# Seven of eight gate tiles of a hybrid encoder block by a seven-product block scheme, and the last head's attention in pieces among the u products (one core)

## The chip, the core and the metric

The kernel runs on one core of a Trainium2 chip. The metric is device time in microseconds of one execution of the whole program. Five engines work side by side, each through its own queue in order: TensorE (PE in the profile, its weight loads PEld), VectorE (DVE), ScalarE (ACT), GpSimd (POOL) and SyncE (SP, which here only issues DMAs). Tiles live in SBUF, and TensorE writes its results into PSUM, which has eight banks of 128 x 512 float32.

## What is computed

One layer of an encoder on a sequence of S = 512 tokens with D = 1024 features, all float32:

```
n = rms_norm(h, norm_mix_pre);  proj = n @ w_in        # 1024 x 7680
z_gmlp (u, v), q, k, v, gates = split(proj)
y_a = u * (w_spatial @ LN(v) + b_spatial)              # after gelu, chunks of 128
y_b = dilated window attention, 3 groups x 4 heads, mixed by softmax denominators
g_a, g_b = split(sigmoid(gates + b_gate))              # 1024 columns each
merged = g_a * (y_a @ w_branch_a) + g_b * (y_b @ w_branch_b)
h = h + rms_norm(merged @ w_out)
h = h + rms_norm(relu(rms_norm(h) @ w_up)**2 @ w_down)
```

## The kernel before

Every large product keeps float32 precision with three fast products. A matrix is split into a rounded high part (type float32r, an ACT copy) and the rest (a DVE subtraction; lines 75 and 76 in `wsplit`, 80 and 81 in `split_into`), and `mm3` (lines 83 to 87) issues high x high, high x low and low x high into one PSUM bank. So one 128-deep step of a product of 128 x 128 weights with 512 moving columns is three matmuls.

The work runs in stages. The input is normed and transposed into `nh`, `nl` (eight slices of 128 features), then v of attention group 0 and of groups 1 and 2 is projected, then q and k of four heads; head h-1 is attended inside the projections of head h (`project_qk`, line 262). `mix(h)` joins the softmax statistics, and `attend(h)` (lines 371 to 415) transposes the probabilities in four rounds through the one PSUM bank with the tag "T", copies them out, and accumulates 12 matmuls of group 0 and the strided ones of the others into the bank "y".

Then comes the part that the change touches. `token_major` for v of the gMLP (line 466) fills the four banks of the tag "acc"; half-way through its text stands `attend(NH - 1)`, the last head. `evac_v` (lines 456 to 464) applies gelu to each of the four banks and norms them. The u loop (lines 468 to 483) makes four feature tiles of 24 matmuls each in the two banks of the tag "S", applies gelu (`gelu2`, lines 447 to 452), multiplies by the spatial product `pg` and splits the result into `yah`, `yal`.

The gate loop (lines 494 to 514) goes over eight column tiles d. For each, two gate products (branches 0 and 1) of 8 x 3 matmuls with 512 moving columns go through a sigmoid with a bias; two branch products of 4 x 3 matmuls are multiplied with the gates and added, and the sum is split into `mh[:, d]`, `ml[:, d]`. Weights come in slabs of 256 columns. After that w_out, w_up and w_down follow; the w_up stage (lines 707 to 738) already uses the seven-product scheme for 14 pairs of column tiles.

The order of instructions on each engine is not the order of the text. A list scheduler places an instruction when its inputs, its buffers and its engine are free in its own time model, the earlier text first. `tc.issue_after(x)` only forbids that TensorE instructions of the block stand ahead of x. A tile waits for its buffer until every reader of the former tile there is done; pools of a closed stack give their SBUF to later pools, which wait for the old tiles in the same way. So the `mpool` of line 489 waits for what the `attn` stack (closed in line 486: `v0h`, `v0l`, `v12` and the probabilities) held.

## Time and profile before

| what | value |
|---|---|
| median of 3 runs (range) | 828.11 us (827.78 to 830.46) |
| the profiled execution's own time | 827.73 us |
| its span, first to last instruction | 826.0 us |
| TensorE busy | 809.8 us (98%) |
| VectorE, ScalarE, GpSimd busy | 493.1 us (60%), 348.9 us (42%), 80.3 us (10%) |
| granted TensorE clock | 1.000 |

In the profile's rows, `L85 PE MATMUL pf<-nh,hi` is a matmul issued by line 85 that writes tile `pf` from `nh` and `hi`; then come the shape, the count, and busy time and mean duration. Matmuls overlap in the pipeline: one of 512 columns lasts 393 ns in its row, but the next starts earlier. What a matmul costs is therefore the distance from one start to the next, read from the timeline or from the count in a window that is wholly busy. A bracket at the end of a timeline row is the idle time ahead of it, and who ended it.

### The profile page before, as it was taken

What the parts mean: (1) busy time and instruction counts of PE and PEld (TensorE: products, weight loads), DVE (VectorE), ACT (ScalarE), POOL (GpSimd) and SP (SyncE); (2) the same over time, 40 slices, a digit from 0 to 9 for tenths busy, and PEclk for the clock granted to TensorE, in tenths of its full rate; (3) what the DMA queues carried; (4) which work ended last, traced back from release to release, by engine and by line L of the source; (5) the groups of instructions that cost most, each with busy time, mean ns of one, the idle gap of its engine ahead of it and who ended that gap; (6) DMA issues with size and microseconds to landing.
All of it is one profiled execution on the core that took longest, in us unless ns stands there. A gap on an engine that the chain in (4) does not pass through costs nothing.

```text
span 826.0 us, 10927 instructions
## 1 busy us (share of the span) xinstructions
PE 809.8 (98%) x4371; PEld 704.8 (85%) x4371; DVE 493.1 (60%) x831; ACT 348.9 (42%) x561; POOL 80.3 (10%) x82
## 2 busy tenths in 40 slices
PE   7999999999999999999999999999999999999997
PEld 5899888888888778888888889999999888888885
DVE  6432788978775637433336579988887533333324
ACT  6322243435344353232326455666666533223312
POOL 2000123232215200000001100000000000000000
PEclk9999999999999999999999999999999999999999
DMA  9433233322213131431436221533333733222202
GB/s 306 137 103 97 67 92 102 85 69 82 74 52 121 60 102 53 152 102 51 153 107 199 102 78 52 153 102 103 103 103 120 263 102 102 89 79 91 100 1 102
DMA packets 70372, 86.90 MB, mean 105 GB/s; under 512 B 2033, under 2 KB 57489, under 8 KB 70322
## 3 DMA queue, kind: packets, MB, share of 16 engines
...
q14 instruction: 16, 0.13, 0.1%
...
## 4 chain that ended last, share of the span: by engine, by line
PE 96%; ACT 1%; DVE 1%; DMA 1%; issue 0%; SPq 0%; DVEq 0%; POOLq 0%; ACTq 0%
PE pf L87 12%; PE pf L86 12%; PE pf L85 12%; PE pacc L699 11%; PE pd L85 9%; PE pd L86 9%; PE pd L87 9%; PE ptp L699 5%; PE pv L85 4%; PE pv L87 4%; PE pv L86 4%; PE py L413 1%; PE psb L313 1%; PE pu L86 1%; PE pu L87 1%; PE pu L85 1%
## 5 line engine op out<-in xcount | busy, mean ns | idle before, releaser
L87 PE MATMUL pf<-nh,lo 128*128 128x512 f32 x352 | 138.2, 393 | 0.0
L86 PE MATMUL pf<-nl,hi 128*128 128x512 f32 x352 | 138.1, 392 | 0.0
L85 PE MATMUL pf<-nh,hi 128*128 128x512 f32 x352 | 137.8, 392 | 0.0
L85 PE MATMUL pd<-hl,hh 128*128 128x512 f32 x224 | 87.1, 390 | 1.0 <-ACT hh L80 1.0
L86 PE MATMUL pd<-hl,hh 128*128 128x512 f32 x224 | 87.2, 389 | 0.0
L87 PE MATMUL pd<-hl 128*128 128x512 f32 x224 | 86.0, 389 | 0.0
L87 PEld LDWEIGHTS pf<-nh,lo 128*128 128x128 f32 x352 | 66.1, 188 | 13.5 <-issue 0.2
L85 PEld LDWEIGHTS pf<-nh,hi 128*128 128x128 f32 x352 | 66.1, 188 | 13.5 <-issue 0.2
L86 PEld LDWEIGHTS pf<-nl,hi 128*128 128x128 f32 x352 | 66.1, 188 | 13.3
L699 PE MATMUL pacc<-nt,hl 128*128 128x256 f32 x504 | 68.2, 280 | 0.4 <-DVE hl L81 0.3
L81 DVE TENSOR_TENSOR hl<-hid,hh 128x512 fp32r<-128x512 f32 x28 | 19.3, 693 | 79.3 <-ACT hh L80 78.9
L699 PEld LDWEIGHTS pacc<-nt,hl 128*128 128x128 f32 x504 | 63.1, 188 | 0.9 <-DVE hl L81 0.5
L254 POOL TENSOR_TENSOR sw<-sw,rope 32x512 f32<-32x512 f32 x24 | 42.3, 1761 | 174.6 <-DVE sw L252 157.5
L80 ACT ACTIVATE hh<-hid 128x512 fp32r<-128x512 f32 x28 | 17.6, 630 | 92.9 <-PE pd L86 92.9
L85 PE MATMUL pv<-hi,nh 128*128 128x512 f32 x128 | 50.9, 402 | 0.4 <-ACT nh L80 0.4
L87 PE MATMUL pv<-hi,nl 128*128 128x512 f32 x128 | 51.2, 401 | 0.0
L86 PE MATMUL pv<-lo,nh 128*128 128x512 f32 x128 | 51.1, 399 | 0.0
L85 PEld LDWEIGHTS pd<-hl,hh 128*128 128x128 f32 x224 | 42.0, 188 | 10.4 <-ACT hh L80 1.4
L87 PEld LDWEIGHTS pd<-hl 128*128 128x128 f32 x224 | 42.0, 188 | 8.7
L86 PEld LDWEIGHTS pd<-hl,hh 128*128 128x128 f32 x224 | 42.0, 188 | 8.6
L81 DVE TENSOR_TENSOR hl<-dnw,hl 128x1024 fp32r<-128x1024 f32 x32 | 39.2, 1226 | 13.8 <-ACT hl L80 13.8
L75 ACT ACTIVATE hi<-qkw 128x1024 fp32r<-128x1024 f32 x24 | 25.4, 1058 | 49.4 <-PE pf L86 25.8
...
## 6 DMA issues: line engine op xcount, KB each, us to landing
upw<-in_w_up_dram SPq DMA_DIRECT2D x16, 1024.0 KB, 5.6
dnw<-in_w_down_dram SPq DMA_DIRECT2D x16, 1024.0 KB, 4.8
qkw<-in_w_in_dram SPq DMA_DIRECT2D x24, 512.0 KB, 4.6
gw<-in_w_in_dram SPq DMA_DIRECT2D x8, 1024.0 KB, 5.2
slab<-in_w_in_dram SPq DMA_DIRECT2D x6, 1024.0 KB, 12.8
wow<-in_w_out_dram SPq DMA_DIRECT2D x4, 1024.0 KB, 4.9
w0raw<-in_w_in_dram SPq DMA_DIRECT2D x4, 512.0 KB, 6.6
uw<-in_w_in_dram SPq DMA_DIRECT2D x2, 1024.0 KB, 5.8
```

What stands on the lines that cost most here:

```text
L75: nc.scalar.activation(hi, raw, AF.Copy)
L80: nc.scalar.activation(hi, src, AF.Copy)
L81: nc.vector.tensor_tensor(lo, src, hi.bitcast(F32), op=ALU.subtract)
L85: nc.tensor.matmul(ps, ah, bh, start=start, stop=False)
L86: nc.tensor.matmul(ps, ah, bl, start=False, stop=False)
L87: return nc.tensor.matmul(ps, al, bh, start=False, stop=stop)
L254: nc.gpsimd.tensor_tensor(sw, sw, rope[:, 1], op=ALU.mult)
L313: nc.tensor.matmul(ps[:, rr, g - 1], got["q", g][:, r], got["k", g][:, r], start=True, stop=True)
L413: nc.tensor.matmul(o, v12[:, g, r, hs], ptb[r // 2][:, r % 2, g], start=False, stop=(r == 3 and g == 1), skip_group_check=True)
L699: nc.tensor.matmul(ps, a[:, j], b[:, j], start=first and not (j or m), stop=(j == KH - 1 and m == 2), skip_group_check=True)
```

## The change

- **Gates.** Tile d = 0 stays as it was. For each d from 1 to 7, the two gate column tiles (branch 1 and branch 0) and the two halves of 256 tokens form a 2 x 2 block product, which is made from seven products of half depth (4 k-steps) with 256 moving columns in place of eight. The weights get four sums (`seven`), the moving side gets four combinations once (`four_sums`, on a rebuilt float32 copy `nf` of the normed input), and PSUM results are combined by DVE and ACT. Product 4 of a pair and its two branch products (`branches`) come after product 6 of the next pair. The branch products use the PSUM banks "T" and "y". Weights come in 128-column pieces.
- **Last head.** `attend` becomes a generator with four yields; the pieces for head 3 are traced after the fourth and the eighth k-step of the u tiles. The u tiles move from the banks "S" to the banks "acc", the spatial products and the small set-up transposes to the banks "S".
- **Memory.** The pool `gpool` moves to the right side, a 160-byte spacer goes, and the scratch for GpSimd's dynamic DMAs is set to 8192 bytes, which leaves that much more per partition for tiles.

```diff
-    spacer(right, 160, "yedge")
...
-        ps = psA.tile([P, S], F32, name="pf", tag=tag, bufs={"acc": 4, "S": 2}[tag])
+        ps = psA.tile([P, S], F32, name="pf", tag=tag, bufs={"acc": 4, "S": 2, "T": 1, "y": 1}[tag])
...
+    def attend_steps(h):
...
             pta_l.append(lo)
+            yield
...
+        turn_b(0)
         for k in range(4):
+            if k == 2:
+                yield
+                turn_b(1)
...
+        yield
         for r in range(4):
...
-    gpool = pool(gst, "gpool")
+    gpool = pool(gst, "gpool", side="right")
...
-    token_major(COL_V, lambda n, k, c: n[:, k, ROT + c * P:ROT + (c + 1) * P], evac_v, lambda: attend(NH - 1))
+    token_major(COL_V, lambda n, k, c: n[:, k, ROT + c * P:ROT + (c + 1) * P], evac_v)
+    KH = KD // 2
+    A, B = slice(0, 256), slice(256, 512)
+    def four_sums(f, tiles):
+        fe, fo = f[:, 0:KD:2], f[:, 1:KD:2]
+        nc.vector.tensor_tensor(fe[:, :, A], fe[:, :, A], fe[:, :, B], op=ALU.subtract)
...
+        for nm, src in ((6, fo[:, :, B]), (5, fe[:, :, A]), (7, fe[:, :, B]), (4, fo[:, :, A])):
+            got[nm] = (tiles(), tiles())
+            split_into(*got[nm], src)
...
+    def seven(raw, sums, split2, split1):
+        raw = raw.rearrange("p (j h) (r c) -> p j (h r) c", h=2, r=2)
+        s = sums()
+        nc.vector.tensor_tensor(s[:, :, 0:4:2], raw[:, :, 1:3], raw[:, :, 0:1].to_broadcast([P, KH, 2, P]), op=ALU.add)
+        nc.vector.tensor_tensor(s[:, :, 3], s[:, :, 2], raw[:, :, 1], op=ALU.add)
+        s12 = split2(s[:, :, 2:4], "s")
+        ar = split2(raw[:, :, 1:3], "r")
+        a12 = split1(raw[:, :, 3])
+        nc.vector.tensor_tensor(s[:, :, 1], s[:, :, 3], raw[:, :, 3], op=ALU.add)
+        s34 = split2(s[:, :, 0:2], "s")
...
+    def product(n, ps, w, moving, first):
+        (wh, wl), (bh, bl) = w[n], moving[n]
+        for j in range(KH):
+            for i, (a, b) in enumerate(((wh, bh), (wh, bl), (wl, bh))):
+                nc.tensor.matmul(ps, a[:, j], b[:, j], start=first and not (j or i), stop=(j == KH - 1 and i == 2), skip_group_check=True)
+    def seven_pairs(n, weights, moving, banks, snap, two, rows, evac, after):
...
+            product(6, Y, w, moving, True)
+            if tail:
+                tail()
+            product(1, X, w, moving, True)
+            p1, z5, u2, u3 = snap("p1", two), snap("z5", 1), snap("u2", 1), snap("u3", 1)
+            nc.scalar.activation(p1, X, AF.Copy)
+            nc.vector.tensor_tensor(u2, Y, p1, op=ALU.add)
+            product(5, Z, w, moving, True)
+            nc.scalar.activation(z5, Z, AF.Copy)
+            product(2, X, w, moving, False)
+            evac(i, c1[:, A], X)
+            product(7, Y, w, moving, False)
+            nc.vector.scalar_tensor_tensor(u3, Y, -1.0, p1, op0=ALU.mult, op1=ALU.subtract)
+            product(3, Z, w, moving, False)
+            nc.vector.tensor_tensor(c1[:, B], Z, u2, op=ALU.add)
+            nc.vector.tensor_tensor(c2[:, B], u3, z5, op=ALU.subtract)
+            def tail(i=i, w=w, Y=Y, p1=p1, c2=c2):
+                product(4, Y, w, moving, False)
+                nc.vector.scalar_tensor_tensor(c2[:, A], Y, -1.0, p1, op0=ALU.mult, op1=ALU.subtract)
+                after(i)
...
+    steps = attend_steps(NH - 1)
...
-            ps = feature_tile(wh, wl, KD, nhn, nln, "S")
+            ps = psA.tile([P, S], F32, name="pf", tag="acc", bufs=4)
+            for k in range(KD):
+                ins = mm3(ps, (wh[:, k], wl[:, k]), (nhn[:, k], nln[:, k]), k == 0, k == KD - 1)
+                if k % 4 == 3 and steps:
+                    with tc.issue_after(ins.ins):
+                        if next(steps, 0) == 0:
+                            steps = None
...
-            pg = psA.tile([P, 4, P], F32, name="pg", tag=("y", "T")[g % 2])
+            pg = psA.tile([P, 4, P], F32, name="pg", tag="S", bufs=2)
...
+    nf = mpool.tile([P, KD, S], F32, name="nf", tag="ml")
...
+    tpool = pool(gp, "tpool", bufs=8)
+    gst.close()
...
+    gapool = pool(gp, "gapool")
...
+    GSTD = 1
...
+            hl = gapool.tile([P, 2, KH, 2, P], F32R, name="ar")
+            split_into(hl[:, 0], hl[:, 1], src)
...
+    def gate_after(i):
+        d = i + GSTD
+        nc.scalar.activation(gs[d][:, 1, B], gs[d][:, 1, B], AF.Sigmoid, bias=cols[:, d:d + 1])
+        nc.scalar.activation(gs[d][:, 0], gs[d][:, 0], AF.Sigmoid, bias=cols[:, 8 + d:9 + d])
+        branches(d)
+    def branches(d):
+        g = gs.pop(d)
+        for br in (1, 0):
+            bhl = gapool.tile([P, 2, 4, P], F32R, name=f"b{br}")
+            split_into(bhl[:, 0], bhl[:, 1], rawb[d][:, br])
+            yh, yl = ((yah, yal), (ybh, ybl))[br]
+            pb = feature_tile(bhl[:, 0], bhl[:, 1], 4, yh, yl, "Ty"[br])
+            nc.vector.tensor_tensor(g[:, 1 - br], pb, g[:, 1 - br], op=ALU.mult)
+        nc.vector.tensor_tensor(g[:, 0], g[:, 0], g[:, 1], op=ALU.add)
+        split_into(mh[:, d], ml[:, d], g[:, 0])
...
+        if d == 0:
+            for k in range(0, KD, 2):
+                nc.vector.tensor_tensor(nf[:, k:k + 2], nhn[:, k:k + 2].bitcast(F32), nln[:, k:k + 2].bitcast(F32), op=ALU.add)
+            nmov = four_sums(nf, lambda: tpool.tile([P, KH, 256], F32R, name="nt", tag="nt"))
+            for n, (kh, half) in {1: (0, A), 2: (1, A), 3: (1, B)}.items():
+                nmov[n] = (nhn[:, kh:KD:2, half], nln[:, kh:KD:2, half])
...
+    seven_pairs(KD - GSTD, gate_weights, nmov, gate_banks, lambda nm, nb: gapool.tile([P, 256], F32, name=nm, bufs=nb), 1,
+                gate_rows, gate_evac, gate_after)
...
-    nc = _bacc.Bacc("TRN2", target_bir_lowering=False, num_devices=1)
+    nc = _bacc.Bacc("TRN2", target_bir_lowering=False, num_devices=1, dynamic_dma_scratch_size=8192)
```

More of the change, by code (lines that the diff above doesn't have):

```diff
@@ L371, in attend @@
     def attend(h):
+        for _ in attend_steps(h):
+            pass
+    def attend_steps(h):
         hs = slice(h * HD, (h + 1) * HD)
@@ L389, in attend, with turn_b @@
             pta_l.append(lo)
+            yield
         ptb = []
-        for r2 in range(2):
+        def turn_b(r2):
             pt = psA.tile([P, 2, 2, P], F32, name="pt", tag="T")
@@ L434, in block_kernel @@
     nc.gpsimd.dma_start(wsp, w_spatial.rearrange("g t s -> t g s"))
-    pt = psA.tile([P, 32], F32, name="ptr", tag="T")
+    pt = psA.tile([P, 32], F32, name="ptr", tag="S", bufs=2)
     nc.tensor.transpose(pt, rows, ident[:32, :32])
@@ L438, in block_kernel @@
     wst = gpool.tile([P, 4, P], F32, name="wst")
-    pt = psA.tile([P, 4, P], F32, name="pt", tag="T")
+    pt = psA.tile([P, 4, P], F32, name="pt", tag="S", bufs=2)
     for g in range(4):
@@ L442, in block_kernel @@
     nc.scalar.activation(wst, pt, AF.Copy)
-    pt = psA.tile([P, 4, P], F32, name="prs", tag="T")
+    pt = psA.tile([P, 4, P], F32, name="prs", tag="S", bufs=2)
     nc.tensor.matmul(pt, onesq, wst, start=True, stop=True)
@@ L464, in evac_v @@
         nc.vector.tensor_scalar(v, v, mv[:, 0:1], r, op0=ALU.subtract, op1=ALU.mult)
-    token_major(COL_V, lambda n, k, c: n[:, k, ROT + c * P:ROT + (c + 1) * P], evac_v, lambda: attend(NH - 1))
+    token_major(COL_V, lambda n, k, c: n[:, k, ROT + c * P:ROT + (c + 1) * P], evac_v)
[4 more added lines that the diff above has]
+        nc.vector.tensor_tensor(fe[:, :, A], fe[:, :, A], fe[:, :, B], op=ALU.subtract)
+        nc.vector.tensor_tensor(fe[:, :, B], fo[:, :, B], fe[:, :, B], op=ALU.subtract)
+        nc.vector.scalar_tensor_tensor(fo[:, :, B], fe[:, :, A], -1.0, fo[:, :, B], op0=ALU.mult, op1=ALU.subtract)
+        nc.vector.scalar_tensor_tensor(fo[:, :, A], fo[:, :, B], -1.0, fo[:, :, A], op0=ALU.mult, op1=ALU.subtract)
+        got = {}
+        for nm, src in ((6, fo[:, :, B]), (5, fe[:, :, A]), (7, fe[:, :, B]), (4, fo[:, :, A])):
+            got[nm] = (tiles(), tiles())
+            split_into(*got[nm], src)
+        return got
@@ new lines, in seven @@
+    def seven(raw, sums, split2, split1):
[8 more added lines that the diff above has]
+        s34 = split2(s[:, :, 0:2], "s")
+        pick = lambda g, i: [z[:, :, i] for z in g]
+        return {1: pick(ar, 0), 2: a12, 3: pick(s34, 1), 4: pick(ar, 1), 5: pick(s12, 0), 6: pick(s12, 1), 7: pick(s34, 0)}
@@ new lines, in product @@
+    def product(n, ps, w, moving, first):
[4 more added lines that the diff above has]
+    def seven_pairs(n, weights, moving, banks, snap, two, rows, evac, after):
+        tail = None
+        for i in range(n):
+            c2, c1 = rows(i)
+            w = weights(i)
+            Y, Z, X = banks()
+            product(6, Y, w, moving, True)
[18 more added lines that the diff above has]
+                after(i)
+        tail()
@@ L483, in block_kernel @@
             split_into(yah[:, g], yal[:, g], tf)
-    gst.close()
     attn.close()
@@ L490, in block_kernel @@
     mh = mpool.tile([P, KD, S], F32R, name="mh")
-    ml = mpool.tile([P, KD, S], F32R, name="ml")
+    nf = mpool.tile([P, KD, S], F32, name="nf", tag="ml")
     gp = ExitStack()
-    gapool = pool(gp, "gapool", bufs=2)
-    for d2 in range(4):
-        raws = [wload([KD, 2 * P], lambda r: [(r, fcols(w_in, COL_G + br * D + d2 * 2 * P, KD, 2 * P))], "gw") for br in range(2)]
-        rawb = wload([2, 4, 2 * P], lambda r: [(r[:, br], w[:, d2 * 2 * P:(d2 + 1) * 2 * P].rearrange("(k p) c -> p k c", p=P))
-                                               for br, w in enumerate((w_branch_a, w_branch_b))], "bw")
-        for j in range(2):
-            d = 2 * d2 + j
-            sl = slice(j * P, (j + 1) * P)
-            tmp = []
-            for br in range(2):
-                wh, wl = wsplit(raws[br][:, :, sl])
-                ps = feature_tile(wh, wl, KD, nhn, nln)
-                sg = gapool.tile([P, S], F32, name=f"sg{br}")
-                nc.scalar.activation(sg, ps, AF.Sigmoid, bias=cols[:, br * 8 + d:br * 8 + d + 1])
-                tmp.append(sg)
-            for br in (1, 0):
-                bh, bl = wsplit(rawb[:, br, :, sl], gapool, tag=f"b{br}")
-                yh, yl = ((yah, yal), (ybh, ybl))[br]
-                pb = feature_tile(bh, bl, 4, yh, yl)
-                nc.vector.tensor_tensor(tmp[br], pb, tmp[br], op=ALU.mult)
-            nc.vector.tensor_tensor(tmp[0], tmp[0], tmp[1], op=ALU.add)
-            split_into(mh[:, d], ml[:, d], tmp[0])
@@ new lines, in block_kernel, with gate_rows, gate_raw @@
+    spacer(gp, 32, "tedge", "left")
+    tpool = pool(gp, "tpool", bufs=8)
+    gst.close()
+    spacer(gp, 224, "gedge", "left")
+    gapool = pool(gp, "gapool")
+    gs, rawb = {}, {}
+    GSTD = 1
+    def gate_rows(i):
+        d = i + GSTD
+        gs[d] = gapool.tile([P, 2, S], F32, name="gs")
+        return gs[d][:, 0], gs[d][:, 1]
+    def gate_raw(d):
+        raw = wload([KD, 2, P], lambda r: [(r[:, :, 1 - br], fcols(w_in, COL_G + br * D + d * P, KD, P)) for br in range(2)], "gw")
+        rawb[d] = gapool.tile([P, 2, 4, P], F32, name="bw")
+        for br, w in enumerate((w_branch_a, w_branch_b)):
+            nc.sync.dma_start(rawb[d][:, br], w[:, d * P:(d + 1) * P].rearrange("(k p) c -> p k c", p=P))
+        return raw
@@ new lines, in gate_weights, with split2, split1 @@
+    def gate_weights(i):
+        raw = gate_raw(i + GSTD)
+        def split2(src, tag):
+            if tag == "s":
+                return wsplit(src)
+            hl = gapool.tile([P, 2, KH, 2, P], F32R, name="ar")
+            split_into(hl[:, 0], hl[:, 1], src)
+            return hl[:, 0], hl[:, 1]
+        def split1(src):
+            hl = gapool.tile([P, 2, KH, P], F32R, name="a12")
+            split_into(hl[:, 0], hl[:, 1], src)
+            return hl[:, 0], hl[:, 1]
+        return seven(raw.rearrange("p k r c -> p k (r c)"), lambda: wpool.tile([P, KH, 4, P], F32, name="s", tag="raw"), split2, split1)
@@ new lines, in gate_banks, with gate_evac @@
+    def gate_banks():
+        return [psA.tile([P, 512], F32, name="pg" + tag, tag=tag, bufs=nb)[:, A] for tag, nb in (("acc", 4), ("acc", 4), ("S", 2))]
+    def gate_evac(i, dst, X):
+        d = i + GSTD
+        nc.scalar.activation(dst, X, AF.Sigmoid, bias=cols[:, d:d + 1])
+    def gate_after(i):
+        d = i + GSTD
+        nc.scalar.activation(gs[d][:, 1, B], gs[d][:, 1, B], AF.Sigmoid, bias=cols[:, d:d + 1])
+        nc.scalar.activation(gs[d][:, 0], gs[d][:, 0], AF.Sigmoid, bias=cols[:, 8 + d:9 + d])
+        branches(d)
@@ new lines, in block_kernel @@
+    for d in range(GSTD):
+        g2 = gate_rows(d - GSTD)
+        raw = gate_raw(d)
+        for br in range(2):
+            ps = feature_tile(*wsplit(raw[:, :, 1 - br]), KD, nhn, nln)
+            nc.scalar.activation(g2[1 - br], ps, AF.Sigmoid, bias=cols[:, br * 8 + d:br * 8 + d + 1])
+        if d == 0:
[4 more added lines that the diff above has]
+                nmov[n] = (nhn[:, kh:KD:2, half], nln[:, kh:KD:2, half])
+            ml = mpool.tile([P, KD, S], F32R, name="ml", tag="ml")
+        branches(d)
```

## The prediction, made before the changed kernel ran

> **What bounds the kernel now.** I read the page's totals and its chain of waits first, then windows over the stages, then the timeline around the edit.

> ```profile
> span 826.0 us, 10927 instructions
> ...
> PE 809.8 (98%) x4371; PEld 704.8 (85%) x4371; DVE 493.1 (60%) x831; ACT 348.9 (42%) x561; POOL 80.3 (10%) x82
> ...
> PE 96%; ACT 1%; DVE 1%; DMA 1%; issue 0%; SPq 0%; DVEq 0%; POOLq 0%; ACTq 0%
> ```

> TensorE is busy for 98% of the span and carries 96% of the chain. So the time is the sum of what the matmuls take plus the few places where TensorE waits; other engines cost only where they make it wait. The profiled execution took 827.73 us, 1.7 us more than its span and 0.4 us under the median of 828.11; I sum against 827.7.

> A busy share doesn't tell what a matmul costs, because matmuls overlap. The step from start to start does. Two windows that are wholly busy, the first in the gate loop, the second in the w_up stage, which already runs seven-product pairs:

> ```profile
> 330.00:430.00 100.00, 100.00 (x437) 81.80 (x436) 38.26 (x49) 29.83 (x41) 1.29 (x3) 1.00 0.34 113
> 540.00:620.00 80.00, 80.00 (x681) 80.00 (x681) 67.55 (x98) 52.88 (x74) 0.00 (x0) 1.00 0.36 106
> ```

> and two rows of the gate loop's timeline, twelve matmuls apart:

> ```profile
> 339.84 0.39 PE L85 MATMUL pf<-nh,hi 128*128 128x512 f32 x1
> ...
> 342.56 0.39 PE L85 MATMUL pf<-nh,hi 128*128 128x512 f32 x1
> ```

> A gate matmul of 512 columns takes (342.56 - 339.84) / 12 = 0.2267 us. One of 256 columns takes 80 / 680 = 0.1177 us (one of the 681 straddles an edge). That is 0.519 of the long one, not half.

> **The gate products.** Per d, the change replaces 2 x 24 = 48 long matmuls, 10.88 us, by 7 products x 4 k-steps x 3 = 84 short ones, 9.88 us. It gains 1.00 us, and over seven pairs **7.0 us**. The d = 0 tile and all 24 branch matmuls per d stay. I take the short step from the w_up stage because there DVE and ACT run about as densely as they will here.

> The second window also shows what bounds the short matmuls: weight loads are busy 80.00 of 80.00 us, against 81.80 of 100 in the gate loop. One load lasts

> ```profile
> L699 PEld LDWEIGHTS pacc<-nt,hl 128*128 128x128 f32 x504 | 63.1, 188 | 0.9 <-DVE hl L81 0.5
> ```

> 188 ns, more than the step of 118, so loads overlap each other or the matmuls. [...]

> **What the pairs put on DVE and ACT.** The groups of the w_up stage, then those of the gate loop:

> ```profile
> L81 DVE TENSOR_TENSOR hl<-s,hl 128x1024 fp32r<-128x1024 f32 x27 | 33.0, 1223 | 6.4 <-ACT hl L80 6.2
> L80 ACT ACTIVATE hl<-s 128x1024 fp32r<-128x1024 f32 x26 | 27.5, 1058 | 29.0 <-PE pacc L699 15.3 <-DVE s L683 10.2 <-DVE s L688 3.2
> ...
> L682 DVE TENSOR_TENSOR s<-upw 128x1024 f32<-128x1024 f32 x13 | 15.9, 1223 | 0.1
> ...
> L688 DVE TENSOR_TENSOR s<-s,upw 128x512 f32<-128x512 f32 x13 | 8.9, 687 | 0.1
> L683 DVE TENSOR_TENSOR s<-s,upw 128x512 f32<-128x512 f32 x13 | 8.9, 685 | 0.0
> L81 DVE TENSOR_TENSOR a12l<-upw,a12h 128x512 fp32r<-128x512 f32 x12 | 8.2, 685 | 0.0
> ...
> L721 DVE TENSOR_TENSOR u<-pacc,p 128x256 f32<-128x256 f32 x14 | 5.9, 420 | 0.1
> ```

> ```profile
> L512 DVE TENSOR_TENSOR sg<-pf,sg 128x512 f32<-128x512 f32 x16 | 11.1, 691 | 20.1 <-PE pf L87 20.1
> ...
> L76 DVE TENSOR_TENSOR lo<-bw,hi 128x512 fp32r<-128x512 f32 x12 | 8.2, 683 | 0.3 <-ACT hi L75 0.3
> L81 DVE TENSOR_TENSOR ml<-sg,mh 128x512 fp32r<-128x512 f32 x7 | 4.9, 693 | 4.2 <-ACT mh L80 4.2
> L513 DVE TENSOR_TENSOR sg<-sg,sg 128x512 f32<-128x512 f32 x7 | 4.8, 687 | 0.0
> ```

> Preparing a pair's weights is 1.22 + 0.69 + 0.69 for the sums, 3 x 1.22 + 0.69 for the low parts: 6.9 us. Five combinations out of PSUM at 0.42 are 2.1. Branch work is 2 x 0.68 + 2 x 0.69 + 0.69 + 0.69 = 4.1. DVE has **13.2 us** per pair. TensorE has 9.88 + 24 x 0.2267 = **15.3 us**. So DVE goes from about 40% to 86% busy and still isn't the bound; the w_up stage keeps its pace with less room, 6.9 + 2.1 = 9.0 us of DVE in 9.88. Cost nothing, with 2.1 us of room per pair as cover; a stage that loses that room pays the overhang. ACT copies at 1.06 us are fewer than DVE's operations: in the window of the w_up stage it was busy 52.88 of 80.

> Loads: gate weights now come in pieces of 128 columns, the form of the q/k loads.

> ```profile
> qkw<-in_w_in_dram SPq DMA_DIRECT2D x24, 512.0 KB, 4.6
> gw<-in_w_in_dram SPq DMA_DIRECT2D x8, 1024.0 KB, 5.2
> ```

> A pair needs two of 512 KB and two branch pieces in 15.3 us, and asks a pair ahead; I cost that at nothing, at worst one landing of 4.6 us for the first pair. The halved DMA scratch touches only GpSimd's queue, whose transfers lie far ahead of their readers: nothing, and no row bounds it better.

> **The u tiles lose a bank.** Before, u's first tile went to a bank "S" and started right behind v:

> ```profile
> 263.81 0.39 PE L87 MATMUL pv<-hi,nl 128*128 128x512 f32 x1
> 264.04 0.39 PE L85 MATMUL pf<-nh,hi 128*128 128x512 f32 x1
> ```

> Now it needs one of the four "acc" banks, all of which hold v until the gelu has read them for the last time (line 452). DVE's timeline:

> ```profile
> 262.94 1.14 DVE L369 TENSOR_SCALAR p<-p,ca 128x256 f32<-128x256 f32 x4
> 264.00 1.28 DVE L450 SCALAR_TENSOR_TENSOR gt<-gt,pv 128x512 f32<-128x512 f32 x2
> 265.90 1.28 DVE L452 SCALAR_TENSOR_TENSOR vln<-gt,pv 128x512 f32<-128x512 f32 x2 [0.62 <-ACT gt L451]
> ```

> The first of the two L452 ends at about 265.90 + 0.64 = 266.5, so TensorE waits **2.5 us** at 264. Queued behind it are all u tiles, and behind those the last head, whose pieces may not pass the fourth k-step. The set-up transposes, in bank "S", can fill at most about 1.3 us of it; a DVE queue in another order adds about one more L450/L452 pair, 1.3 us. Bounds 1.2 and 3.8; I take 2.5, straight from the rows.

> **The last head moves.** Its 16 transposes, 12 + 16 matmuls, five ACT and three DVE operations (no DMA) stay the same in number. Before, they ran late although the probabilities were final at 262.94 + 1.14 = 264.1; the tail made TensorE wait:

> ```profile
> 288.92 0.60 PE L384 MATMUL pt<-ident,p 128*128 128x128 f32 x4
> ...
> 301.75 0.66 PE L395 MATMUL pt<-ident,p 128*128 128x128 f32 x4 [0.31 <-ACT ptb L397]
> ...
> 305.66 1.16 PE L478 MATMUL pg<-wst,vln 128*128 128x128 f32 x8 [0.52 <-DVE ybl L81]
> 308.03 0.49 PE L85 MATMUL pf<-ybh,hi 128*128 128x512 f32 x1 [1.21 <-ACT hi L75]
> ```

> Together 2.04 us. With the head done among the u tiles, the two gate products of d = 0 (10.9 us) lie between the u tiles and the first branch product, so I let all **2.0 us** go. What is late next is the first pair's weights, below. If that cover is gone, the 2.0 us come back.

> **The start of the pairs.** Four rebuilding adds, four sums and four low parts of 128 x 1024 on the moving side are 12 x 1.22 = 14.7 us of DVE, the first pair's weights 6.9: 21.6 us. They have to fit beside the gelu and d = 0.

> ```profile
> 264.00:300.00 36.00, 36.00 (x166) 29.25 (x165) 21.80 (x42) 15.68 (x23) 8.93 (x9) 1.00 0.39 123
> 300.00:313.00 13.00, 10.96 (x77) 9.45 (x76) 6.90 (x11) 7.99 (x12) 0.00 (x0) 1.00 0.06 18
> ...
> 503.00:520.00 17.00, 16.23 (x134) 15.66 (x133) 16.83 (x23) 8.44 (x14) 0.00 (x0) 1.00 0.21 61
> 520.00:640.00 120.00, 119.71 (x1007) 119.04 (x1006) 100.29 (x143) 79.11 (x110) 1.11 (x2) 1.00 0.36 109
> ```

> Before, DVE was busy 28.7 of the 49 us from 264 to 313: 20.3 are free, 1.3 fewer than needed. Against that, product 6 needs only part of it, and the list scheduler can put branch products ahead. The w_up stage started the same way: DVE busy 16.83 of 17.00 us, TensorE short of 0.77, then 0.29 over the next 120 us. I take **1.5 us**. The bounds are 0 and half of the free time unusable, because `nf` lies where v and the probabilities lay and can't be written until the last head is done: 11.5 us.

> **Sum.** 827.7 - 7.0 - 2.0 + 2.5 + 1.5 = **822.7 us**, 0.6% faster. A measurement of this kernel can't tell less than about 0.3% from no change.

> **Rivals.** (a) *Both new waits are covered*: set-up work and a faster gelu hide the bank, the scheduler hides the start. 827.7 - 7.0 - 2.0 = 818.7. For it: TensorE lost only 0.29 us in 120 in the established pairs. Against it: nothing else in the text may use TensorE at 264, as the rest waits for "acc" too. (b) *The start of the pairs starves*: DVE's combinations wait at the head of its queue for the last head's release, and u's own gelu and the first weights queue behind them. At 11.5 us in place of 1.5 the time is 832.7. It makes the kernel slower than before from 6.5 us on (827.7 - 821.2). For it: 20.3 us free against 21.6 wanted, and one engine's strict order. Against it: the head should be done by about 285, and the w_up start lost 0.77. (c) *Single buffers stall every pair*: tile `ar` has one buffer, read last by product 4, so the next pair's copy (1.06) and low part (1.22) start only then, and product 1 waits. It decides only if the 5.4 us of branch matmuls don't stand between the two; then 7 x 2.3 = 16 us more, 838.7. Against it: the text puts them there. (d) *Short matmuls pay a whole weight load each*, not overlapped: 84 x 0.188 = 15.8 us a pair, 4.9 more than now, and with 34.4 in place of the gain some 864. [...] The step of 118 ns speaks flatly against it. (e) *The gain is eaten by waits*: the old ones stay, the bank costs its upper bound and the start 2.5 us: 827.7 - 7.0 + 3.8 + 2.5 = 827.0. Each is possible, and all three together need a scheduler that gains nothing from the new order.

> **How the numbers follow.** Forecast 0.65, its own range 820 to 825.5; (a) 0.15; (b) 0.10; (c) 0.05; (d) 0.01; (e) 0.04. Range 817.5 to 826.5: it takes in the forecast and (a), which hold 0.80, and leaves out the rest. Faster by over 0.3% (below 825.2): 0.62 of the forecast and (a), 0.77. Slower: (c), (d) and most of (b), and a little for both waits at their upper bounds together, 0.13. Same: the rest, 0.10.

> **What would show it.** Right: 588 short matmuls at 0.118 us between about 310 and 420, about 15.3 us from pair to pair; an idle TensorE of 1 to 4 us ahead of the first u matmul, released by DVE line 452; the waits for `ptb`, `ybl` and the branch weights gone; DVE some 85% busy in the pairs. Wrong: idle TensorE once in every pair (c); an idle stretch over 5 us ahead of product 6 (b); a short step above 0.125; or no wait at the u tiles (a).

## The result, and the profile after

| | before | after |
|---|---|---|
| median of 4 runs (range) | 827.94 us (827.53 to 830.46) | 833.98 us (833.34 to 836.53) |
| ratio, 95% interval | | 1.0074 [1.0053, 1.0095] |
| profiled execution, its span | 827.73, 826.0 us | 833.34, 831.6 us |
| v's last matmul to w_out's first | 263.81 to 431.52 = 167.71 us | 265.42 to 438.09 = 172.67 us |
| w_out's first to the end | 394.4 us | 393.5 us |

The change makes the kernel 0.7% slower, where 0.6% faster was forecast. The loss lies between v and w_out: 5.0 us. Another 1.6 us of the two spans' difference arose ahead of the first q product, which the change doesn't touch. That moment came at 81.2 us in before, 81.6 in e3 and 82.0 to 84.4 in the other fifteen profiles. Two things move it: the start of v's first product (9.96 us in before, 11.03 in after) and the end of a first stretch in which long matmuls step at 0.43 us in place of 0.23 (12.79 and 14.20). Kernels that hold the change have early values too (10.15 in e9, 13.90 in e14), so a cause in the change is neither shown nor excluded.

The page of after, its first line, its engines and the chain by engine:

```profile
span 831.6 us, 11602 instructions
...
PE 805.1 (97%) x4623; PEld 712.2 (86%) x4623; DVE 547.2 (66%) x913; ACT 370.0 (45%) x600; POOL 81.1 (10%) x83
...
PE 87%; DVE 6%; ACT 2%; DMA 2%; issue 1%; SPq 1%; DVEq 0%; POOLq 0%; POOL 0%; ACTq 0%
```

TensorE did less (805.1 us against 809.8) and the kernel took longer. The share of the chain that runs through VectorE went from 1% to 6%. The view of waits names the places (us in total, times, longest):

```profile
PE pf L85 <- DVE vln L463: 2.4, 1, 2.4
...
PE pgacc L511 <- DVE nt L81: 2.2, 1, 2.2
PE pd L85 <- DVE gs L631: 2.0, 1, 2.0
...
PE pgacc L511 <- DVE lo L76: 1.3, 2, 0.7
...
PE pgS L511 <- DVE ar L81: 0.7, 1, 0.7
PE pgacc L511 <- ACT gs L640: 0.5, 1, 0.5
PE pf L85 <- ACT b L80: 0.5, 1, 0.5
PE pgacc L511 <- DVE u L531: 0.5, 1, 0.5
...
PE pgS L511 <- ACT ar L80: 0.4, 1, 0.4
```

Four groups: the u tiles wait for their bank (2.4); the start of the pairs (2.2 + 0.5 + 0.4 + 0.5, and 0.3 in two short ones, 4.0); two pairs wait for weights (1.3); the last pair and the end of the gates wait (0.7 + 0.5 + 2.0). The old tail's waits for `ptb`, `ybl` and the branch weights are gone. The two waits for weights, at 372.90 and 404.69 us, each follow a stop of VectorE for a load, here of 2.09 us and later, at 397.61, of 2.12:

```profile
365.08 1.23 DVE L497 TENSOR_TENSOR s<-gw 128x1024 f32<-128x1024 f32 x1 [2.09 <-DMA gw<-in_w_in_dram]
```

Now TensorE's timeline at the start of the pairs:

```profile
312.02 0.38 PE L511 MATMUL pgacc<-nt,hi 128*128 128x256 f32 x1 [0.23 <-ACT nt L80]
314.58 0.58 PE L511 MATMUL pgacc<-nt,hi 128*128 128x256 f32 x1 [2.18 <-DVE nt L81]
...
315.17 0.63 PE L511 MATMUL pgacc<-nt,hi 128*128 128x256 f32 x2
315.60 0.41 PE L511 MATMUL pgacc<-nt,lo 128*128 128x256 f32 x1
...
319.49 1.08 PE L511 MATMUL pgacc<-nt,hi 128*128 128x256 f32 x4 [0.54 <-ACT gs L640]
```

Besides the brackets, look at the steps: from 315.17 to 315.60 two matmuls take 0.43 us, 0.215 each instead of 0.118. The windows show why (us, busy of PE, PEld, DVE, ACT, POOL, then the granted clock):

```profile
265.40:311.50 46.10, 43.66 (x229) 36.35 (x228) 40.49 (x68) 20.80 (x31) 9.47 (x11) 1.00 0.25 68
303.00:313.30 10.30, 9.17 (x41) 7.22 (x39) 10.30 (x13) 5.57 (x7) 0.00 (x0) 1.00 0.18 53
314.57:317.98 3.41, 3.40 (x16) 3.40 (x17) 3.41 (x5) 1.58 (x2) 0.00 (x0) 0.50 0.00 0
323.00:433.00 110.00, 107.92 (x729) 99.47 (x728) 77.70 (x116) 49.33 (x79) 0.14 (x1) 1.00 0.42 120
```

For 3.41 us the clock stood at one half, right behind the idle 2.18 us; by half its length that costs 1.7 us more. And VectorE was busy for all of the 10.30 us ahead of the splits that product 6 wants. Once the pairs run, it is at 77.70 of 110, 71%. Its order at that place:

```profile
295.96 4.63 DVE L643 TENSOR_TENSOR nf<-nh,nl 128x1024 f32<-128x1024 f32 x4
...
311.02 1.23 DVE L497 TENSOR_TENSOR s<-gw 128x1024 f32<-128x1024 f32 x1
312.16 1.23 DVE L487 SCALAR_TENSOR_TENSOR nf<-nf 128x1024 f32<-128x1024 f32 x1
313.30 2.37 DVE L81 TENSOR_TENSOR nt<-nf,nt 128x1024 fp32r<-128x1024 f32 x2
315.56 0.70 DVE L498 TENSOR_TENSOR s<-s,gw 128x512 f32<-128x512 f32 x1
```

Line 643 rebuilds the normed input in the place `nf`, with which all work on the moving side begins; the last head's last matmul (line 424) had ended at 295.56 us. The sums `s` of lines 497 and 498 here are the second pair's weights, in front of or among the splits `nt` of the first pair's moving side. On ScalarE, one of the halves of `s` stands ahead of the evictions of the d = 0 tile. These hold the bank "acc" of the third product, which starts at 319.49 us behind 24 short matmuls:

```profile
316.38 1.06 ACT L75 ACTIVATE hi<-s 128x1024 fp32r<-128x1024 f32 x1 [1.90 <-DVE s L498]
317.46 1.28 ACT L640 ACT_TABLE_LOAD   x1
318.75 1.26 ACT L640 ACTIVATE gs<-pf,cols 128x512 f32<-128x512 f32 x2
```

**Theory after the comparison:** VectorE can't finish what stands between v and the pairs in the time that u and one old-scheme tile give it, and the change starts all of it late by the u wait. **Rivals:** the u bank is the cause and everything behind it only follows; or ScalarE's order is; or the short matmuls themselves cost more than counted.

### The profile page after: what moved, and what is told of

The parts are those of the page before. It is cut to its first block, busy times and chain, and to the rows that moved or that the text cites. A ratio compares the mean times of both kernels' runs of the same rounds, so it can differ in the third digit from the quotient of the medians.

```text
span 831.6 us, 11602 instructions
## 1 busy us (share of the span) xinstructions
PE 805.1 (97%) x4623; PEld 712.2 (86%) x4623; DVE 547.2 (66%) x913; ACT 370.0 (45%) x600; POOL 81.1 (10%) x83
## 4 chain that ended last, share of the span: by engine, by line
PE 87%; DVE 6%; ACT 2%; DMA 2%; issue 1%; SPq 1%; DVEq 0%; POOLq 0%; POOL 0%; ACTq 0%
PE pacc L835 11%; PE pd L85 9%; PE pd L87 9%; PE pd L86 9%; PE pf L85 8%; PE pf L87 7%; PE pf L86 7%; PE pgacc L511 5%; PE ptp L835 4%; PE pv L87 3%; PE pv L86 3%; PE pv L85 3%; PE pgS L511 2%; DMA xt<-in_x_dram 1%; DVE lo L76 1%
## 5 line engine op out<-in xcount | busy, mean ns | idle before, releaser
L85 PE MATMUL pf<-nh,hi 128*128 128x512 f32 x240 | 95.0, 396 | 2.4 <-DVE vln L463 2.4
L87 PE MATMUL pf<-nh,lo 128*128 128x512 f32 x240 | 94.3, 393 | 0.0
L86 PE MATMUL pf<-nl,hi 128*128 128x512 f32 x240 | 94.3, 393 | 0.0
L85 PE MATMUL pd<-hl,hh 128*128 128x512 f32 x224 | 87.1, 390 | 1.0 <-ACT hh L80 1.0
L87 PE MATMUL pd<-hl 128*128 128x512 f32 x224 | 86.0, 389 | 0.0
L81 DVE TENSOR_TENSOR hl<-hid,hh 128x512 fp32r<-128x512 f32 x28 | 19.3, 693 | 79.3 <-ACT hh L80 78.9
L80 ACT ACTIVATE hh<-hid 128x512 fp32r<-128x512 f32 x28 | 17.6, 630 | 92.9 <-PE pd L86 92.9
L85 PEld LDWEIGHTS pf<-nh,hi 128*128 128x128 f32 x240 | 45.1, 188 | 11.4 <-DVE vln L463 2.9
L87 PEld LDWEIGHTS pf<-nh,lo 128*128 128x128 f32 x240 | 45.1, 188 | 8.9
L86 PEld LDWEIGHTS pf<-nl,hi 128*128 128x128 f32 x240 | 45.1, 188 | 8.5
L85 PE MATMUL pv<-hi,nh 128*128 128x512 f32 x128 | 51.1, 403 | 1.3 <-ACT nh L80 1.3
L87 PE MATMUL pv<-hi,nl 128*128 128x512 f32 x128 | 51.1, 401 | 0.0
L85 PEld LDWEIGHTS pd<-hl,hh 128*128 128x128 f32 x224 | 42.0, 188 | 10.2 <-ACT hh L80 1.4
L87 PEld LDWEIGHTS pd<-hl 128*128 128x128 f32 x224 | 42.1, 188 | 8.8
L81 DVE TENSOR_TENSOR hl<-dnw,hl 128x1024 fp32r<-128x1024 f32 x32 | 39.2, 1226 | 13.8 <-ACT hl L80 13.8
L75 ACT ACTIVATE hi<-qkw 128x1024 fp32r<-128x1024 f32 x24 | 25.4, 1058 | 49.4 <-PE pf L86 25.7
## 6 DMA issues: line engine op xcount, KB each, us to landing
upw<-in_w_up_dram SPq DMA_DIRECT2D x16, 1024.0 KB, 5.5
dnw<-in_w_down_dram SPq DMA_DIRECT2D x16, 1024.0 KB, 4.9
qkw<-in_w_in_dram SPq DMA_DIRECT2D x24, 512.0 KB, 4.8
gw<-in_w_in_dram SPq DMA_DIRECT2D x16, 512.0 KB, 5.1
slab<-in_w_in_dram SPq DMA_DIRECT2D x6, 1024.0 KB, 12.9
wow<-in_w_out_dram SPq DMA_DIRECT2D x4, 1024.0 KB, 4.9
w0raw<-in_w_in_dram SPq DMA_DIRECT2D x4, 512.0 KB, 7.7
uw<-in_w_in_dram SPq DMA_DIRECT2D x2, 1024.0 KB, 5.1
```

Of the source, the lines that this page charges most:

```text
L75: nc.scalar.activation(hi, raw, AF.Copy)
L80: nc.scalar.activation(hi, src, AF.Copy)
L81: nc.vector.tensor_tensor(lo, src, hi.bitcast(F32), op=ALU.subtract)
L85: nc.tensor.matmul(ps, ah, bh, start=start, stop=False)
L86: nc.tensor.matmul(ps, ah, bl, start=False, stop=False)
L87: return nc.tensor.matmul(ps, al, bh, start=False, stop=stop)
```

## The experiments

All are timed beside the kernel before (medians 828.3 to 828.9 us); ratios are to it.

**Half of the scratch and no spacer, in the kernel before (e3).**

```diff
-    spacer(right, 160, "yedge")
...
-    nc = _bacc.Bacc("TRN2", target_bir_lowering=False, num_devices=1)
+    nc = _bacc.Bacc("TRN2", target_bir_lowering=False, num_devices=1, dynamic_dma_scratch_size=8192)
```

> The kernel before with only the halved dynamic DMA scratch and without the 160-byte spacer. The changed kernel started its first fast matmul at 11.0 us in place of 10.0. If the scratch or the addresses cause that, this kernel takes 1 to 1.6 us more than before (829 to 829.5) and its first matmul of v starts near 11. If the start varies from execution to execution, it takes what the kernel before takes, within 0.3%.

Measured 826.47 us, 0.9976 [0.9965, 0.9987]. A branch matmul in the groups of before and of e3 (same line, same operands):

```profile
L85 PE MATMUL pf<-ybh,hi 128*128 128x512 f32 x32 | 12.8, 399 | 1.2 <-ACT hi L75 1.2
```

```profile
L85 PE MATMUL pf<-ybh,hi 128*128 128x512 f32 x32 | 12.6, 393 | 1.2 <-ACT hi L75 1.2
```

The 192 branch matmuls step at a median of 227 ns in place of 232 (means 226.7 and 233.8 without the steps behind waits). From u's first matmul to w_out's, e3 takes 165.9 us and the kernel before 167.5. So about 1.6 us of the change's effect is a gain that the prediction had at nothing. TensorE, VectorE and ScalarE run the same instructions in the same order in both traces, so what changed for them is where tiles lie; whether the scratch or the spacer does it was not separated. The first product of v starts at 10.21 us in its profile, nearer to the 9.96 of before than to the 11.03 of after.

**The head alone (e4): the changed kernel with the old gate loop.**

```diff
-    for d in range(GSTD):
...
-    seven_pairs(KD - GSTD, gate_weights, nmov, gate_banks, lambda nm, nb: gapool.tile([P, 256], F32, name=nm, bufs=nb), 1,
...
+    for d2 in range(4):
+        raws = [wload([KD, 2 * P], lambda r: [(r, fcols(w_in, COL_G + br * D + d2 * 2 * P, KD, 2 * P))], "gw") for br in range(2)]
...
```

> The changed kernel with the old gate loop: only the last head in pieces, the moved banks and the pool on the other side are left. If the waits add up, the bank wait of 2.4 us comes and the 2.0 us of the old tail go: 828, no change from before, with no clock drop. If the head's move costs VectorE order as well, it is 830 or more; if the old tail had more in it than its 2.0 us of idle time, 826 or less.

Measured 827.80 us, 0.9983 [0.9968, 0.9998]. The old tail's waits are gone and the u wait of 2.44 us is there, with a half-speed window behind it at 268.1 us (u's first matmul steps 0.60 us there, in after 0.33). The head in pieces gives and takes about the same, also against e3, which has the same scratch and no spacer (0.9976, inside this interval).

**The gates alone (e7): the head as before, u in "S".**

```diff
-    token_major(COL_V, ..., evac_v)
+    token_major(COL_V, ..., evac_v, lambda: attend(NH - 1))
...
-    steps = attend_steps(NH - 1)
+    steps = None
...
-            ps = psA.tile([P, S], F32, name="pf", tag="acc", bufs=4)
+            ps = psA.tile([P, S], F32, name="pf", tag="S", bufs=2)
...
-            pg = psA.tile([P, 4, P], F32, name="pg", tag="S", bufs=2)
+            pg = psA.tile([P, 4, P], F32, name="pg", tag=("y", "T")[g % 2])
```

> The changed kernel with the last head attended as before, in one piece half-way through v, and the banks of u as before; the seven-product gates, the right-hand pool and the scratch are left. If the gate products carry their 7.0 us and the losses are the start of the pairs, the late weights and the end bank (about 9 us with one clock drop), it takes 829 to 831. If the combinations of the moving side depend on the last head's end, which now comes later, the start gets worse by 5 us or more: 834 or above.

Measured 838.08 us, 1.0111 [1.0089, 1.0132]. This order was another than I meant: nearly the whole head came ahead of u, whose first matmul started at 278.4 us, so the time says little of the gates. Its trace says something of the start of the pairs. VectorE stood 2.48 us for line 424, the head's last matmul, and began the rebuilding adds at 282.62 us, 4.3 us behind u's first matmul in place of 27.7 in after. Product 6 then waited for no split at all, with one old-scheme tile and only 37.6 us from u's first matmul to it, in after 43.3. What was left is a wait of 3.45 us for the evictions of line 640, with 6.83 us at half clock around it (short matmuls step at 0.213 us behind the wait).

**The u bank (e1, e5).** e1 only exchanges the tags of u's tiles and the spatial products:

```diff
-            ps = psA.tile([P, S], F32, name="pf", tag="acc", bufs=4)
+            ps = psA.tile([P, S], F32, name="pf", tag="S", bufs=2)
...
-            pg = psA.tile([P, 4, P], F32, name="pg", tag="S", bufs=2)
+            pg = psA.tile([P, 4, P], F32, name="pg", tag="acc", bufs=4)
```

> The changed kernel with the u tiles back in the banks S and the spatial products in the banks acc. If the waits add up, the 2.4 us of idle TensorE ahead of the first u matmul go and the time falls from 833.3 to about 831. If VectorE bounds the stretch from v to the first pair, the u matmuls start 2.4 us earlier but the idle time ahead of the first product 6 grows by as much, and the time stays within 1 us of 833.3.

Measured 840.35 us, 1.0139 [1.0113, 1.0164]: a miss. The set-up transposes share "S" and were placed ahead of u, where TensorE stood 6.87 us for their rows:

```profile
274.28 0.28 PE L447 MATMUL ptr<-ident,rows 32*128 32x32 f32 x1 [6.87 <-DMA rows<-in_norm_mlp_pre_dram]
```

e5 puts the set-up into "acc" as well and behind the first u group:

```diff
+            if g == 0:
+                with tc.issue_after(ins.ins):
+                    set_up()
```

> The changed kernel with the u tiles in the banks S again, the spatial products and the set-up transposes in the banks acc, and the set-up transposes held behind the first u tile so that they can't stand ahead of it as they did in e1. If the waits add up, the 2.4 us of idle TensorE at 265 go and with them any clock drop there: 831.5 or a little less. If VectorE bounds the stretch up to the first pair, the first product 6 waits 2 us longer than the 2.4 us it waits now, and the time stays at 833 to 834.

Measured 833.02 us, 1.0051 [1.0034, 1.0068]. TensorE's timeline of e5:

```profile
265.95 0.39 PE L87 MATMUL pv<-hi,nl 128*128 128x512 f32 x1
266.18 0.39 PE L85 MATMUL pf<-nh,hi 128*128 128x512 f32 x1
...
312.87 0.58 PE L514 MATMUL pgacc<-nt,hi 128*128 128x256 f32 x1 [3.40 <-ACT nt L80]
314.76 0.58 PE L514 MATMUL pgacc<-nt,hi 128*128 128x256 f32 x1 [1.31 <-ACT nt L80]
```

The u wait is gone, and product 6 comes hardly earlier: its second wait ends 48.8 us behind v's last matmul, in after 49.2. The wait moved to the splits and grew, another of 1.42 us for the evictions of line 646 follows, and the clock was at half for 10.24 us (mean granted clock 0.992, in after 0.997). VectorE's rebuilding adds began at 297.23 us, after 1.22 us of waiting for line 424. So the u bank isn't the cause: the stretch from v to the pairs has another bound.

**The end of the gates (e2, e6).** Both are to give w_out's first accumulator another bank, e2 by the order of the tags:

```diff
-    accs = [[psB.tile([P, 512], F32, name="pd", tag=tg, bufs=4) for _ in range(2)] for tg in ("tp", "acc", "acc", "acc")]
+    accs = [[psB.tile([P, 512], F32, name="pd", tag=tg, bufs=4) for _ in range(2)] for tg in ("acc", "tp", "acc", "acc")]
```

> The changed kernel with the first two output banks of w_out taken from the tag acc instead of tp, so that they don't reuse the bank that the last branch product holds. If that bank is what the 2.0 us at the end of the gates wait for, the time falls by about 2 us to 831.3, and w_out starts behind product 4. If the split of the w_out weights or of the last merged tile is as late, less than 0.7 us is won.

and e6 by exchanging the tiles once they are placed:

```diff
+    accs[0], accs[1] = accs[1], accs[0]
```

> The changed kernel with the output banks of the first two row blocks of w_out exchanged, the order of allocation kept, so that the first sums of w_out really lie in another bank than the last branch product (in e2 the pool had laid out the new tag over the same bank). If the bank is what the 2.0 us wait for, they fall to under 0.7 us and the time to about 832; if the w_out weights are as late, nothing changes.

e2: 836.53 us, 1.0093 [1.0067, 1.0118]. The wait of 2.00 us stayed, so its first tile seems to have landed in the same bank, and its profile has two half-speed windows (mean granted clock 0.994). e6: 834.99 us, 1.0075 [1.0056, 1.0095]. The wait ahead of w_out is gone, but its profile has three half-speed windows (269.1, 316.9, 323.8 us; mean granted clock 0.993) against one in after's (0.997). From u to w_out it took 170.92 us against 169.84: two windows more, 3.4 us, and 2.3 us less of waiting. The gain shows in the time only where these are gone, below.

**Two old-scheme tiles (e8).**

```diff
-    GSTD = 1
+    GSTD = 2
```

> The changed kernel with two gate tiles done the old way (d = 0 and 1) and six pairs. It gives up 1.0 us of the product gain and gains 16 us of TensorE work as cover for the start of the pairs. If VectorE's backlog is what the first pair waits for, the 4 us of idle time there and the clock drop of 1.7 us go: 829 to 830. If the wait comes from something that moves along (late weights, a buffer), it takes 834 to 835.

Measured 828.46 us, 1.0002 [0.9990, 1.0014]: 5.5 us less than after, with one pair's saving given up. Its two longest waits from u to w_out:

```profile
PE pf L85 <- DVE vln L463: 2.4, 1, 2.4
PE pd L85 <- DVE gs L631: 2.0, 1, 2.0
```

The waits at the start of the pairs and both waits for weights within the pairs are gone; the last pair's 0.7 and 0.5 us stay. Another 10.9 us of long matmuls ahead of the pairs is enough for VectorE.

**Two old-scheme tiles with the banks of e5 (e9), of e6 (e10), and of both (e11).**

> Two gate tiles by the old scheme (as in e8, 828.46 us, 0.15 us from the kernel before in the ratio) and the u products' bank from the pair of S with the set-up transposes behind the first u group (as in e5). In e8 the 2.44 us at u stayed, with a clock window at half speed behind it (1.7 us), and nothing was waited for at the start of the pairs. Theory (VectorE is behind only where one old-scheme tile stands ahead of the pairs; a second tile's 96 long matmuls give it the slack): the u wait and the half-speed window go and do not come back at the pairs: 2.44 + 0.28 refill = 2.7 us less, up to 4.4 with the window, so 824.0 to 825.8 us. Rival (the stretch from v to the pairs is VectorE-bound with two tiles too): the wait comes back ahead of the first product 6, as in e5, and the time stays at 827.5 to 829.

> As e8 with the first two accumulators of the output product exchanged (as in e6, where the 2.00 us ahead of that product went, but the time did not). Theory (the end wait is a bank held by the last branch sum, with nothing else late behind it): 2.00 + 0.28 us go, and the half-speed window that e8's profile had behind it, so 824.5 to 826.2 us. Rival (what follows the wait is late anyway, since the last tile of the gates is needed by the output product's later steps, so that the wait moves): 828 to 829, with an idle time of about 2 us within the first matmuls of the output product.

> e9 and e10 together. Theory: both savings add, 828.5 - 2.7 - 2.3 = 823.5 us, and down to about 821.5 where the half-speed windows go with the waits; this is below the kernel before (828.3) and below e3 (826.5, the addresses alone). Rival (each wait only covers another): no better than the better one of e9 and e10, 824.5 or above.

e9: 825.00 us, 0.9956 [0.9942, 0.9969]. e10: 825.61 us, 0.9963 [0.9951, 0.9976]. e11: **821.48 us, 0.9917 [0.9904, 0.9931]**, faster than both kernels. The savings against e8 are 3.5 and 2.9 us, and 7.0 us together. Each is more than its bare wait, since the half-speed windows behind the waits (269.6 and 433.5 us in e8) go as well: the granted clock is 0.994 to 0.997 in e8's ten executions and 0.998 to 0.999 in e11's four. e11's waits between u and w_out, and its window from u to the first product 6:

```profile
PE pgS L514 <- DVE ar L81: 0.7, 1, 0.7
PE pgacc L514 <- DVE u L534: 0.5, 1, 0.5
```

```profile
266.40:320.40 54.00, 54.00 (x277) 45.31 (x276) 49.35 (x75) 29.90 (x43) 8.72 (x11) 1.00 0.29 77
```

TensorE is busy for all 54.00 us, with VectorE at 49.35. With one old-scheme tile the stretch has 10.9 us less of TensorE (268.25 to 311.51 in after, 43.3 us), while on VectorE only the second tile's low parts fall away, two of 1.22 us. By this estimate some 47 us of VectorE's work stand against 43.3, and its share doesn't fit.

**VectorE relieved of the rebuilding adds (e12).**

```diff
-                nc.vector.tensor_tensor(nf[:, k:k + 2], nhn[:, k:k + 2].bitcast(F32), nln[:, k:k + 2].bitcast(F32), op=ALU.add)
+                nc.scalar.activation(nf[:, k:k + 2], nhn[:, k:k + 2].bitcast(F32), AF.Copy)
```

> The changed kernel with one old-scheme tile; the four additions that rebuild the normalised rows (4.63 us of VectorE at 296 us) are replaced by four ScalarE copies of the high halves: the low halves are left out of the moving sums, so that part of the gates' products is less exact. Theory (VectorE's backlog sets the start of the pairs): VectorE gets 4.63 us, so the 2.18 us ahead of the first product 6 goes with the half-speed window behind it, and most of the 1.6 us of waits after the second product: 834.0 - 2.5 - 1.7 and up to 1.5 more, 828.3 to 830 us, with the 2.44 us at u and the 2.00 us at the end unchanged. Rival (ScalarE's order, its sigmoid table load and the evictions behind it, sets the start): the idle time of about 4 us at 311 to 322 us stays and the time is 833 to 835.

Measured 839.31 us, 1.0128 [1.0115, 1.0142]: outside what either expected. TensorE's two waits in e12:

```profile
316.93 0.39 PE L511 MATMUL pgacc<-nt,hi 128*128 128x256 f32 x1 [0.71 <-DVE nt L81]
323.55 1.38 PE L511 MATMUL pgacc<-nt,hi 128*128 128x256 f32 x4 [5.07 <-ACT gs L640]
```

The wait for the splits went from 2.41 us in after (0.23 and 2.18) to 0.71, as the theory has it. The wait for the evictions went from 0.54 to 5.07, and 6.83 us at half clock from 321.3 on came with it (short matmuls step at 0.213 us behind the wait). VectorE's first sum and ScalarE's timeline in e12:

```profile
302.91 1.22 DVE L484 TENSOR_TENSOR nf<-nf 128x1024 f32<-128x1024 f32 x1 [3.10 <-ACT nf L643]
```

```profile
298.99 3.89 ACT L643 ACTIVATE nf<-nh 128x1024 f32<-128x1024 f32 x4
...
320.44 1.06 ACT L75 ACTIVATE hi<-s 128x1024 fp32r<-128x1024 f32 x1 [2.30 <-DVE s L498]
321.52 1.28 ACT L640 ACT_TABLE_LOAD   x1
322.81 1.27 ACT L640 ACTIVATE gs<-pf,cols 128x512 f32<-128x512 f32 x2
```

Most of the freed 4.63 us is idle: VectorE stands 3.10 us for the copies, which begin at 298.99, and its first sum comes only 0.6 us earlier than in after (303.49), or 1.9 counted from v's last matmul, which came 1.3 us later in this execution. The evictions stand on ScalarE behind a half of the second pair's sums, which VectorE now makes later, and come at 322.81 in place of 318.75. So both theories hold a part: VectorE's work sets the wait for the splits, and ScalarE's order, which hangs on VectorE's, the one for the evictions.

**The second pair behind the splits (e13).**

```diff
+            if nm == 4:
+                lead.append(ins.ins)
...
+        with tc.issue_after(lead[0]) if i == 1 else nullcontext():
```

`lead[0]` is VectorE's last split of `nt`, and the block under it is the call of `seven` for the second pair. As `lead[0]` runs on VectorE, it is VectorE's instructions of the block that stay behind it: the second pair's first sum starts at 317.24 us.

> The changed kernel; VectorE's and ScalarE's instructions that prepare the second pair's weights are queued behind the last of the splits of the moving sums (in the changed kernel two of them, 1.23 and 0.70 us, stand among the splits, and the sigmoid evictions of the first tile stand behind one of their halves on ScalarE). Theory (what is in front of the splits in VectorE's order is the price, not the stage's sum of work): the 2.18 us ahead of the first product 6 becomes about 0.95, short of what turned the clock down, and the waits for the evictions go: 834.0 - 1.2 - 1.7 - 0.6 = 830.5 us, 829.5 to 832. Rival (VectorE has too much to do until the second pair, whatever the order): the second pair then waits for its own weights, about 2 us at 325 to 335 us, and the time is 833 to 835.

Measured 831.72 us, 1.0036 [1.0024, 1.0049], 2.3 us less than after. TensorE's waits there:

```profile
311.93 0.39 PE L515 MATMUL pgacc<-nt,hi 128*128 128x256 f32 x1 [0.22 <-ACT nt L80]
313.36 0.39 PE L515 MATMUL pgacc<-nt,hi 128*128 128x256 f32 x1 [1.04 <-DVE nt L81]
317.87 0.39 PE L515 MATMUL pgS<-nh,ar 128*128 128x256 f32 x1 [1.64 <-ACT ar L80]
```

Ahead of product 6 the wait went from 2.41 to 1.26 us as expected, and the wait for the evictions is gone. But 1.64 us for `ar` took part of it back (0.45 in after). Order is worth about half of the wait for the splits; the rest is work. Part of the 2.3 us is clock: all five executions of e13 were granted 0.997, of after's four one 0.997 and the others 0.993 to 0.994.

**One old-scheme tile with everything mended (e14), and no seven-product gates with the u bank mended (e15).** e14 joins the edits of e5, e6 and e13; e15 those of e4 and e5.

> One old-scheme tile, the u products' bank and the output product's first bank exchanged as in e11, and the order of e13. Theory (a second old-scheme tile is needed for VectorE's backlog as soon as u starts 2.4 us earlier): e5's 833.0 us less 2.3 at the end and less 1.9 to 3.5 at the start of the pairs, 827 to 829 us, with 1.5 to 3.5 us idle left ahead of the first product 6: behind e11's 821.5. Rival (order alone was the price): no wait above 1 us at the start of the pairs, and the seventh pair's saving of 1 us comes on top: 820 to 822 us.

> No seven-product gates at all: the head in four pieces (e4, 827.8 us) with the u products' bank from the pair of S and the set-up transposes behind the first u group. Theory (with the old gates nothing on VectorE is late behind u): the 2.44 + 0.28 us go, and the half-speed window of 1.7 us with them: 823.2 to 825.2 us; then e11's 821.5 leaves 2 to 3.5 us for the six seven-product pairs, of the 6.0 that their matmul count gives. Rival (the wait only covers VectorE work that the first gate tile needs too): 827 to 828 us with the idle time at the first gate tile.

e14: 826.91 us, 0.9981 [0.9971, 0.9990]. TensorE stands 2.26 and 1.40 us at the first two matmuls of product 6:

```profile
310.44 0.39 PE L518 MATMUL pgacc<-nt,hi 128*128 128x256 f32 x1 [2.26 <-ACT nt L80]
312.22 0.58 PE L518 MATMUL pgacc<-nt,hi 128*128 128x256 f32 x1 [1.40 <-DVE nt L81]
```

with a window of 6.83 us at half speed from 310.9 (granted clock 0.50). One tile isn't enough cover even in this order, and the rival fell; the time lies just under the theory's 827 to 829. e15: 824.03 us, 0.9946 [0.9932, 0.9960], with no wait from u to w_out. So e11's six pairs, with the bank exchange at the end that they make necessary, are worth 2.6 us in the medians. Their stage, u's first matmul to w_out's, in e15 and in e11:

```profile
265.09 0.39 PE L85 MATMUL pf<-nh,hi 128*128 128x512 f32 x1
...
427.87 0.39 PE L85 MATMUL pd<-hi,mh 128*128 128x512 f32 x1
```

```profile
266.49 0.39 PE L85 MATMUL pf<-nh,hi 128*128 128x512 f32 x1
...
426.04 0.39 PE L85 MATMUL pd<-hi,mh 128*128 128x512 f32 x1
```

162.78 against 159.55 us, 3.23 less. e11's two waits are 1.25 us of idle time, and 1.8 with the longer steps from start to start around them. Without them the pairs would save 5.0 us, 0.84 a pair.

## Why the prediction failed, step by step

- **The start of the pairs: the first step that failed.** I took 1.5 us and put it down to 21.6 us of work against 20.3 us of VectorE's free time, with the excuse that product 6 needs only part of it. It cost 4.0 us of idle TensorE and 1.7 us of half clock, 5.7 together. Rival (b) had the mechanism, at the price of its lower half. Two things were wrong. Free time was counted over the whole stretch, but the chain could start only when the last head freed `nf`'s place, and VectorE's rebuilding adds start at 296 us; I had assumed a head that is done by 285. Where VectorE stood idle for that release, it was line 424 that ended the wait (e5, e7), and with the release at 282.6 the wait for the splits was gone (e7). And in both engines' order the second pair's weights stand among the first pair's splits: e13 gets 2.3 us back by that order alone. That a stage of the same scheme (w_up) started with 0.77 us was no measure: there nothing had to be rebuilt, and the first sum started 12.8 us ahead of the first pair (490.41 and 503.25), here 8.0 us (303.49 and 311.51). With 5.7 in place of 1.5 the prediction's sum gives 826.9 us.
- **Costs put at nothing, the second step that failed: the pairs and their end.** The two waits for weights, 1.35 us, and the last pair's `ar`, `u` and the bank of w_out's first accumulator, 3.25 us: 4.6 us in all, which brings the sum to 831.5. The text never asked who reads the last bank ahead of w_out; taking that wait away was worth 2.9 us (e8 to e10). Ahead of each wait for weights VectorE had stood some 2.1 us for the loads that the prediction put at nothing. No run moved the loads, so this cause is not shown by a test: the two waits are absent with two old-scheme tiles (e8 to e11), but also in e1, e5 and e14, where VectorE waits for loads as well.
- **The u bank.** Taken at 2.5, measured 2.44 us. The mechanism held. But it was no separate term of the sum: with the wait taken away, product 6 came hardly earlier (e5), so bank and start share one bound. Where VectorE has cover it counts, 3.5 us with its window (e8 to e9).
- **The old tail.** Its 2.0 us went as predicted.
- **The gate products.** 588 short matmuls at 0.118 us came true, rival (d) did not. That weight loads set this step, as the prediction read it, no run tested. The 7.0 us did not come through whole. By the steps, 288 long matmuls at 0.2267 us against 504 short ones at 0.1184 are 5.6 us for e11's six pairs. Against e15, e11 kept 3.2: the last pair's two waits took 1.8, and branch matmuls beside short ones 0.6 (their mean step is 229.7 ns in e11 and 226.7 in e15, 192 of them).
- **VectorE in the pairs.** 71% busy, not 86%, in part because the 13.2 us added up durations that overlap: two splits of 1.23 us take 2.37 together in the row at 313.30. Rival (c) did not happen in steady state, but once, in the last pair. There twelve short matmuls, and no branch products, stand between product 4, which reads `ar`, and product 1, which wants the next `ar`; VectorE's low part starts at 425.58 us and TensorE waits 0.73 us at 426.86. Every profile of a kernel with pairs has this wait.
- **Scratch and spacer.** Put at nothing; the addresses gave 1.6 us (e3).

The sum again, with what the two profiles show between v's last matmul and w_out's first. The seven pairs' matmuls, by their steps, give -6.6 us, the addresses -1.6, and branch matmuls beside short ones +0.4. Idle time gives +8.9 (10.97 against 2.04), and the half clock +1.7. The longer steps around the waits give some +1.9: the u wait moved TensorE by 2.7 us for 2.44 of idle time. That is +4.7 of the measured 5.0 us. The beginning adds 1.6, and w_out to the end takes 1.0 off; that last stretch took 393.4 to 394.5 us in all these profiles but e8's, with the change and without it.
